# Output projection of a streaming-encoder block: additions moved between VectorE, ScalarE and GpSimd, two buffer pools merged, half of the weight sums traced later

## The chip, the cores and the metric

The kernel runs on one core of a Trainium2 chip. Its time is device microseconds of one execution. TensorE (PE) does the matrix products, VectorE (DVE), ScalarE (ACT) and GpSimd (POOL) the elementwise work, and SyncE (SP) issues nearly all transfers. Each engine works through its own list of instructions in the order in which the compiler has put them, and an instruction that waits holds everything behind it on the same engine.

## The reference, cut to what matters

One layer (depth 1) on a sequence of 2048 tokens with 1024 channels, all in float32:

```
mod = silu(c) @ ada_w + ada_b;  shift, scale, gate = split(mod, 3)
h   = rms_norm(x, norm_pre_w) * (1 + scale) + shift
z   = h @ w_in                                  # 1024 -> 6144 columns
pool_out = multiscale_pool(u) * silu(g_pool)    # 1024 channels
hgrn_out = rms_norm(hgrn2(q, f, i)) * silu(g_h) # 1024 channels, 8 heads
y   = concat(pool_out, hgrn_out) @ w_out        # 2048 -> 1024
out = x + gate * rms_norm(y, norm_post_w)
```

The change concerns the last two lines: the product with w_out, its two halves of the sum over the 2048 channels, the norm of y, and the addition of x.

## The kernel before, in words

Every large product is done in float32 quality from two rounded parts of each operand (`hi` and `lo`, made by `part`, L127: a ScalarE copy that rounds, then a VectorE subtraction), three matmuls for each product of parts. On top of that each block of two by two is computed with seven products instead of eight. `quad` (L356) does one such block: seven calls of `product` (L349), each 12 matmuls of 128 by 128 by 512, into three PSUM banks X, Z and Y, and seven additions that combine the banks into four results. The first copy of X goes to `c21` (L361). The first use of bank Z is copied by ScalarE into `c22` and `c21` is added by GpSimd (L368, L369). The others are VectorE additions of a bank to a tile (L372, L377, L380, L383). X itself is returned and left to the caller. The three banks (tag `ps_mm`) are shared by successive quads, so the next quad's first product waits until X has been read.

The kernel has these stages. A first part prepares the inputs. Then 48 steps, 24 for each half of the sequence, compute the columns of w_in head by head (`fq_step`, `hv_step`) and pool group by pool group (`pool_step`), with the attention units in between, and store the result in a scratch tensor `mix`. At last comes the output projection (from L844): 16 quads, eight with the pool half of the channels (`g` = 0, the first pass), whose results go to a scratch tensor `ypart`, and eight with the other half (`g` = 1, the second pass). A quad makes 256 rows of y, two tiles of 128 rows.

For each quad `mix_granule` (L743) loads 256 rows of `mix` into the one buffer `mraw` and makes seven operands (`m`, tag `w`, six buffers) with GpSimd sums (L758 to L766) and `part`. It is traced one quad ahead. The seven matching operands of w_out are made once for each pass by `load_out` (L718): 14 loads into `oraw` (tag `st`, two buffers), some from w_out itself, some from the scratch tensors `wos[0]` and `wos[1]`, and 28 pairs of a ScalarE and a VectorE instruction.

The sums of w_out that stand in `wos[g]` are made by `out_sums` (L702) in eight calls for each pass. One call loads two blocks of w_out into the tile `x` (tag `x1`, one buffer in all), scales them on ScalarE (L710), makes four GpSimd sums (L712 to L715) and stores the result (L716). The same single buffer `x1` serves `second_sums` in the first half, the gate's row in `gate_row` (L465), and at last the tile `gnb` that holds that row on all partitions (L844, L845). In the second half of the steps all 16 calls are traced, one with each `fq` and each `hv` step (L834), first the eight of pass 0, then `gate_row` (after head 3), then the eight of pass 1.

In the second pass each quad loads two tiles `yp` from `ypart` (L856) and adds them: VectorE adds X and its part (L867), GpSimd the other three quarters (L872; VectorE in the last quad). ScalarE sums the squares of a row tile (L877), GpSimd makes the reciprocal root (L111, L112), VectorE multiplies by it and by the gate's row (L881) and adds x (L882), and SP stores the result (L886). The tiles `yp` and `xf` (the x to be added) share three buffers (tag `px`).

The order of the instructions on each engine is not written by hand: a planner takes the traced program, gives earlier lines the higher priority, and puts on each engine, in a simulated timeline, the first instruction in priority that it thinks ready. An instruction traced late runs early if what it needs is free. The places marked `high_priority` are put ahead. Transfers are in the same way put in one order on SP.

Of the kernel before, what the change touches and what calls it, by code (L numbers as in the profile page):

```python
# [11 lines left out]
F32 = mybir.dt.float32  # L12
# [4 lines left out]
ALU = mybir.AluOpType  # L17
# [3 lines left out]
P = 128  # L21
D = 1024
# [5 lines left out]
BLK = 512  # L28
# [16 lines left out]
def build(nc, tc, a):  # L45
# [4 lines left out]
    out = a["out"][0]  # L50

    with tc.tile_pool(name="dram", bufs=1, space=DRAM) as dram, \
# [8 lines left out]
        gnrow = dram.tile([1, D], F32, name="gnrow")  # L61
# [72 lines left out]
        wsp = wsp_cm.__enter__()  # L134
# [13 lines left out]
        for m in (2, 4, 8, 16):  # L148
            n = 64 // m
# [14 lines left out]
        S = {}  # L164
# [190 lines left out]

        def quad(W, c12, c21, c22, begin=None):  # L356

            X, Z, Y = bank("mm"), bank("mm"), bank("mm")
# [8 lines left out]
            with tc.high_priority():  # L367
                nc.scalar.copy(c22, Z)  # L368
                nc.gpsimd.tensor_tensor(c22, c22, c21, ALU.add)  # L369
            product(Y, W[2], S["S2"], True)  # L370
# [347 lines left out]
        def load_out(g):  # L718

            r = {}  # L720
            for name, t in (("A11", None), ("S1", 0), ("S2", 3), ("A12", None), ("S3", 1), ("S4", None), ("A22", 2)):
                r[name] = []
                for j in range(2):
                    raw = fin[0].tile([P, 2, BLK], F32, name="oraw", tag="st", bufs=2)
                    hi, lo = s_tile("hi"), s_tile("lo")
# [85 lines left out]
        for i, step in enumerate(steps):  # L811
# [20 lines left out]
            if half == 0 and what == "pool" and n in (2, 4):  # L832
                second_sums(HEADS - 4 + n // 2 + 1)
            if half == 1 and what != "pool":  # L834
                out_sums(n // 4, n % 4, int(what == "hv"))
            if half == 1 and what == "hv" and n == 3:
# [6 lines left out]

        gn = wsp.tile([P, D], F32, name="gnb", tag="x1", bufs=1)  # L844
        nc.sync.dma_start(gn, gnrow[0].partition_broadcast(P))  # L845
        todo = [(g, p_) for g in range(2) for p_ in range(T // P // 2)]
        M = nxt
        for i, (g, p_) in enumerate(todo):
            if p_ == 0:
                S.update(O if g == 0 else load_out(1))  # L850
            nxt = mix_granule(*todo[i + 1]) if i + 1 < len(todo) else None
            y = [fin[0].tile([P, D], F32, name="y", tag="y", bufs=4) for _ in range(2)]
            if g:
                parts = [fin[0].tile([P, D], F32, name="yp", tag="px", bufs=3) for _ in range(2)]
                for t in range(2):
                    nc.sync.dma_start(parts[t], ypart[2 * p_ + t])  # L856
            X = quad(M, y[0][:, BLK:], y[1][:, 0:BLK], y[1][:, BLK:])
            M = nxt
            if g == 0:
                with tc.high_priority():  # L860
                    nc.scalar.copy(y[0][:, 0:BLK], X)
                for t in range(2):
                    nc.sync.dma_start(ypart[2 * p_ + t], y[t])
                continue
            final = i == len(todo) - 1
            with tc.high_priority():
                nc.vector.tensor_tensor(y[0][:, 0:BLK], X, parts[0][:, 0:BLK], ALU.add)  # L867
            for t in range(2):
                ts = slice((2 * p_ + t) * P, (2 * p_ + t + 1) * P)
                for n in ((1,), (1, 0))[t]:  # L870
                    ns = slice(n * BLK, (n + 1) * BLK)
                    (nc.vector if final else nc.gpsimd).tensor_tensor(y[t][:, ns], y[t][:, ns], parts[t][:, ns], ALU.add)  # L872
                xt = fin[0].tile([P, D], F32, name="xf", tag="px", bufs=3)
                nc.sync.dma_start(xt, x[ts])
# [4 lines left out]
                for n in range(2):  # L879
                    ns = slice(n * BLK, (n + 1) * BLK)  # L880
                    nc.vector.scalar_tensor_tensor(y[t][:, ns], y[t][:, ns], ss, gn[:, ns], ALU.mult, ALU.mult)  # L881
                    nc.vector.tensor_tensor(y[t][:, ns], y[t][:, ns], xt[:, ns], ALU.add)  # L882
                    if final:
                        nc.sync.dma_start(out[ts, ns], y[t][:, ns])
# [20 lines left out]
```

## Time and profile before

| what | value |
|---|---|
| median of 3 runs | 1822.91 us (1819.11 to 1823.12) |
| profiled execution, its own time | 1825.83 us |
| its span, first to last instruction | 1824.2 us |
| PE busy | 1650.4 us, 90% |
| DVE busy | 1118.2 us, 61% |
| POOL busy | 714.9 us, 39% |
| ACT busy | 645.0 us, 35% |
| mean granted TensorE clock | 0.951 |

Shares are of the span. "Idle before" an instruction is time in which its engine did nothing, and the name behind it is what ended the wait. The granted clock is a share of TensorE's full clock of 2.4 GHz: it takes two levels, full and half, and a mean between them over a stretch says how much of the stretch was at half. L numbers are lines of the kernel before.

### The profile page before, as it was taken

How to read it: one execution, taken by the hardware profiler on the slowest of the kernel's cores; microseconds unless marked ns; L12 is line 12 of the kernel's file. 1: busy time of each engine (PE TensorE's matmuls, PEld its weight loads, DVE VectorE, ACT ScalarE, POOL GpSimd, SP SyncE). 2: the span in 40 equal slices, each digit the busy share in tenths (PEclk: the TensorE clock that was granted, in tenths of full speed). 3: DMA queues.
4: the chain of work that ended last, by engine and by line, in shares of the span. 5: the costliest groups of instructions: out<-in, count | busy, mean ns of one | idle time of the engine just before them, and what ended most of it. 6: DMA issues, size and time to landing. Idle time of an engine off the chain costs nothing. (4 is left out here: it accounts for less than half of the span.)

```text
span 1824.2 us, 31561 instructions
## 1 busy us (share of the span) xinstructions
PE 1650.4 (90%) x12249; PEld 1302.8 (71%) x12249; DVE 1118.2 (61%) x1754; ACT 645.0 (35%) x1417; POOL 714.9 (39%) x924
## 2 busy tenths in 40 slices
PE   7779898999999699889998999989999899988896
PEld 6557676777777477677776877768787668866675
DVE  5496576676676466865545434445544874567776
ACT  4654243434443334443122222322122342343232
POOL 1374354547364627532212213432121233325563
PEclk8789999999999799999999999989999999999898
DMA  9636564667565647797532546554554563263454
GB/s 340 224 128 215 173 220 171 217 213 238 170 213 193 185 164 249 248 329 259 199 128 95 183 156 202 187 195 160 178 174 145 166 221 127 105 219 126 171 187 174
DMA packets 221475, 348.66 MB, mean 191 GB/s; under 512 B 45009, under 2 KB 152590, under 8 KB 221326
## 3 DMA queue, kind: packets, MB, share of 16 engines
q1 hardware_dynamic: 221240, 346.62, 56.5%
q8 instruction: 97, 1.59, 0.4%
q14 instruction: 52, 0.43, 0.1%
q10 hardware_dynamic: 86, 0.03, 0.0%
HBM read 203.99 MB, written 142.61 MB: 190 GB/s over the span
## 5 line engine op out<-in xcount | busy, mean ns | idle before, releaser
L353 PE MATMUL ps_mm<-hi,w 128*128 128x512 f32 x2304 | 786.6, 410 | 41.2 <-ACT ue L368 6.0
L353 PEld LDWEIGHTS ps_mm<-hi,w 128*128 128x128 f32 x2304 | 444.6, 194 | 149.1 <-ACT ue L368 7.1
L353 PE MATMUL ps_mm<-lo,w 128*128 128x512 f32 x1152 | 465.9, 405 | 12.3 <-DVE lo L130 9.1
L353 PE MATMUL ps_mm<-hi,m 128*128 128x512 f32 x896 | 292.8, 405 | 32.5 <-ACT m L129 9.4
L353 PEld LDWEIGHTS ps_mm<-lo,w 128*128 128x128 f32 x1152 | 224.4, 195 | 59.2 <-DVE lo L130 11.9
L353 PEld LDWEIGHTS ps_mm<-hi,m 128*128 128x128 f32 x896 | 174.5, 195 | 80.1 <-ACT m L129 11.9
L130 DVE TENSOR_TENSOR w<-wraw,w 128x512 fp32r<-128x512 f32 x168 | 141.8, 851 | 102.7 <-ACT w L129 94.6
L603 DVE TENSOR_TENSOR qk<-qk,tcn 128x512 f32<-128x512 f32 x192 | 148.7, 774 | 60.6 <-PE ps_lv L632 40.8
L353 PE MATMUL ps_mm<-lo,m 128*128 128x512 f32 x448 | 179.8, 402 | 2.4 <-DVE lo L736 1.8
L129 ACT CAST w<-wraw 128x512 fp32r<-128x512 f32 x168 | 101.9, 620 | 214.2 <-DMA wraw<-w_in 70.3
L353 PE MATMUL ps_mm<-hi,wpair 128*128 128x512 f32 x384 | 132.3, 406 | 5.1 <-DVE sg L501 4.7
L353 PEld LDWEIGHTS ps_mm<-lo,m 128*128 128x128 f32 x448 | 87.9, 196 | 21.9 <-DVE lo L736 3.0
L111 POOL TENSOR_SCALAR ss<-ss 128x4 f32<-128x4 f32 (+2 forms) x60 | 22.5, 375 | 187.1 <-ACT og L685 114.6
L611 PEld LDWEIGHTS ps_lv<-qk 128*32 128x32 f32 x4096 | 49.4, 113 | 55.2 <-issue 39.9
L353 PEld LDWEIGHTS ps_mm<-hi,wpair 128*128 128x128 f32 x384 | 72.9, 191 | 21.0 <-DVE sg L501 4.8
L611 PE MATMUL ps_lv<-qk 128*32 128x16 f32 x4096 | 63.7, 186 | 17.9 <-DVE qk L603 17.2
L130 DVE TENSOR_TENSOR m<-mraw,m 128x512 fp32r<-128x512 f32 x64 | 60.9, 963 | 30.8 <-ACT m L129 30.8
L324 POOL TENSOR_TENSOR wraw<-wraw 128x512 f32<-128x512 f32 x24 | 32.4, 1352 | 113.8 <-DMA wraw<-w_in 46.3
L353 PE MATMUL ps_mm<-lo,wpair 128*128 128x512 f32 x192 | 76.3, 397 | 0.0
L591 DVE COPY_PREDICATED diag<-mask,ps_lv 128x64 f32<-128x64 uint8 x128 | 30.8, 241 | 67.0 <-PE ps_lv L611 66.1
L554 POOL TENSOR_TENSOR tcn<-tcn 128x128 f32<-128x128 f32 (+4 forms) x160 | 65.7, 410 | 9.2
L554 POOL TENSOR_TENSOR tcn<-f 128x256 f32<-128x256 f32 x32 | 23.3, 727 | 114.0 <-ACT f L544 57.8
(279 smaller groups left out, 2640.8 us busy)
## 6 DMA issues: line engine op xcount, KB each, us to landing
wsd<-w SPq DMA_DIRECT2D x168, 512.0 KB
w<-wsd SPq DMA_DIRECT2D x120, 512.0 KB
wpair<-wsd SPq DMA_DIRECT2D x24, 1024.0 KB
wraw<-w_in SPq DMA_DIRECT2D x40, 512.0 KB
mraw<-mix SPq DMA_DIRECT2D x32, 512.0 KB
ada<-ada_w SPq DMA_DIRECT2D x16, 512.0 KB
mix<-g SPq DMA_DIRECT2D x32, 256.0 KB
mix<-sg SPq DMA_DIRECT2D x32, 256.0 KB
```

The costliest lines, as they stand in the source:

```text
L111: nc.gpsimd.tensor_scalar(ss, ss, inv, EPS, ALU.mult, ALU.add)
L129: nc.scalar.copy(hi, raw)
L130: nc.vector.tensor_tensor(lo, raw, hi.bitcast(F32), ALU.subtract)
L324: nc.gpsimd.tensor_tensor(B11, B12, B11, ALU.subtract)
L353: nc.tensor.matmul(ps, w[:, a_, k], s[k][b_], start=start and k == a_ == b_ == 0, stop=k == KH - 1 and a_ == 1, skip_group_check=not start)
L554: nc.gpsimd.tensor_tensor(dst, sv[:, :, 0], sv[:, :, 1], ALU.mult)
L591: nc.vector.copy_predicated(dst, mk, view(data, 0, [(16, NC_), (m, n), (1, m)]))
L603: nc.vector.tensor_tensor(dst, dst, t_, ALU.mult)
L611: nc.tensor.matmul(ps[q * 32:(q + 1) * 32, c * 16:(c + 1) * 16], K[:, t:t + 32], view(Q, t + m, [(2 * m, 16 // m), (1, m)]), start=True, s ...
```

## The change

- `quad` gets a flag `out`. With it, bank Z's first sum is one VectorE addition from the bank; without it, ScalarE copy and GpSimd addition as before. Only the 16 quads of the output projection set it.
- In both passes X is now copied to y by ScalarE. In the second pass the part of `ypart` for that quarter is added later, with the others, and all four quarter additions are on VectorE. The order of quarters is 0, 1 for the first row tile and 1, 0 for the second.
- The addition of x is on GpSimd, and on VectorE in the last quad only.
- `oraw` (two buffers) and `px` (three) become one tag with five buffers of the same size.
- `out_sums`: the second half's `hv` steps trace the eight calls of pass 0 (four before `gate_row`, four after it). The eight calls of pass 1 are traced in the quads of the first pass. `gnb` is taken at the start of the second pass.

```diff
-        def quad(W, c12, c21, c22, begin=None):
+        def quad(W, c12, c21, c22, begin=None, out=False):
...
-                nc.scalar.copy(c22, Z)
-                nc.gpsimd.tensor_tensor(c22, c22, c21, ALU.add)
+                if out:
+                    nc.vector.tensor_tensor(c22, Z, c21, ALU.add)
+                else:
+                    nc.scalar.copy(c22, Z)
+                    nc.gpsimd.tensor_tensor(c22, c22, c21, ALU.add)
...
-                    raw = fin[0].tile([P, 2, BLK], F32, name="oraw", tag="st", bufs=2)
+                    raw = fin[0].tile([P, 2, BLK], F32, name="oraw", tag="px", bufs=5)
...
-            if half == 1 and what != "pool":
-                out_sums(n // 4, n % 4, int(what == "hv"))
+            if half == 1 and what == "hv":
+                out_sums(0, n % 4, n // 4)
...
-        gn = wsp.tile([P, D], F32, name="gnb", tag="x1", bufs=1)
-        nc.sync.dma_start(gn, gnrow[0].partition_broadcast(P))
...
-                S.update(O if g == 0 else load_out(1))
+                S.update(load_out(1) if g else O)
+            if g and p_ == 0:
+                gn = wsp.tile([P, D], F32, name="gnb", tag="x1", bufs=1)
+                nc.sync.dma_start(gn, gnrow[0].partition_broadcast(P))
...
-                parts = [fin[0].tile([P, D], F32, name="yp", tag="px", bufs=3) for _ in range(2)]
+                parts = [fin[0].tile([P, D], F32, name="yp", tag="px", bufs=5) for _ in range(2)]
...
-            X = quad(M, y[0][:, BLK:], y[1][:, 0:BLK], y[1][:, BLK:])
+            X = quad(M, y[0][:, BLK:], y[1][:, 0:BLK], y[1][:, BLK:], out=True)
             M = nxt
+            with tc.high_priority():
+                nc.scalar.copy(y[0][:, 0:BLK], X)
             if g == 0:
-                with tc.high_priority():
-                    nc.scalar.copy(y[0][:, 0:BLK], X)
+                out_sums(1, p_ % 4, p_ // 4)
...
-            with tc.high_priority():
-                nc.vector.tensor_tensor(y[0][:, 0:BLK], X, parts[0][:, 0:BLK], ALU.add)
...
-                for n in ((1,), (1, 0))[t]:
+                for n in (t, 1 - t):
                     ns = slice(n * BLK, (n + 1) * BLK)
-                    (nc.vector if final else nc.gpsimd).tensor_tensor(y[t][:, ns], y[t][:, ns], parts[t][:, ns], ALU.add)
-                xt = fin[0].tile([P, D], F32, name="xf", tag="px", bufs=3)
+                    nc.vector.tensor_tensor(y[t][:, ns], y[t][:, ns], parts[t][:, ns], ALU.add)
+                xt = fin[0].tile([P, D], F32, name="xf", tag="px", bufs=5)
...
-                    nc.vector.tensor_tensor(y[t][:, ns], y[t][:, ns], xt[:, ns], ALU.add)
+                    (nc.vector if final else nc.gpsimd).tensor_tensor(y[t][:, ns], y[t][:, ns], xt[:, ns], ALU.add)
```

## Rows read from the trace of the kernel before

**Rows 1.** Stretches: us, busy us of PE PEld DVE ACT POOL, PEclk, DMA share, GB/s.
```profile
760.00:831.00 71.00, 63.92 (x300) 52.04 (x301) 48.60 (x76) 35.31 (x75) 25.32 (x34) 0.95 0.90 320
...
1110.00:1220.00 110.00, 95.73 (x864) 73.47 (x863) 51.63 (x96) 31.92 (x80) 48.32 (x62) 0.91 0.60 198
1220.00:1400.00 180.00, 179.82 (x1515) 143.87 (x1514) 85.85 (x159) 40.95 (x104) 35.97 (x57) 1.00 0.51 171
...
1457.00:1501.00 44.00, 38.59 (x148) 28.69 (x147) 33.56 (x46) 20.48 (x36) 13.41 (x10) 0.92 0.66 216
1501.00:1596.00 95.00, 95.00 (x421) 78.69 (x420) 47.92 (x58) 31.07 (x56) 33.82 (x26) 1.00 0.33 122
1596.00:1645.00 49.00, 40.94 (x170) 32.19 (x169) 34.73 (x47) 22.90 (x41) 12.78 (x10) 0.97 0.61 204
1645.00:1815.00 170.00, 147.77 (x588) 116.15 (x587) 126.14 (x148) 50.90 (x91) 93.38 (x83) 0.93 0.49 170
```

**Rows 2.** Waits from 1110 to 1220 us: who for whom, us, times, longest.
```profile
ACT x L710 <- DMA x<-w_out: 59.8, 8, 13.3
...
PE ps_mm L353 <- DVE sg L501: 4.7, 1, 4.7
```

**Rows 3.** ScalarE in order of time, 1114 to 1136 us: start, us, instruction, [idle before].
```profile
1131.89 1.36 ACT L710 ACTIVATE x<-x,vec 128x512 f32<-128x512 f32 x2 [13.32 <-DMA x<-w_out]
...
1133.85 0.57 ACT L368 COPY ue<-ps_mm 128x512 f32<-128x512 f32 x1
```

**Rows 4.** All of L710: duration least/median/most in ns, first and last start.
```profile
L710 ACT ACTIVATE x<-x,vec x32: 704/722/751, 698.1 to 1209.9; 128x512 f32<-128x512 f32 x32
```

**Rows 5.** SyncE's transfers in order of issue, 1186 to 1222 us.
```profile
1215.74 0.37 SPq L716 DMA_DIRECT2D wos<-x  x1
...
1219.58 0.33 SPq L845 DMA_DIRECT2D gnb<-gnrow  x1
```

**Rows 6.** Waits of TensorE from 1608 us to the end.
```profile
PE ps_mm L353 <- ACT m L129: 9.4, 6, 2.8
PE ps_mm L353 <- DVE y L372: 9.0, 4, 4.3
PE ps_mm L353 <- DVE y L867: 8.7, 2, 6.3
```

**Rows 7.** Groups of instructions from 1350 us: busy us, mean ns | idle before, releasers.
```profile
L881 DVE SCALAR_TENSOR_TENSOR y<-y,ss,gnb 128x512 f32<-128x512 f32 x32 | 38.6, 1240 | 5.2 <-POOL ss L112 5.2
L872 POOL TENSOR_TENSOR y<-y,yp 128x512 f32<-128x512 f32 x21 | 32.3, 1540 | 32.6 <-DVE y L383 25.1 <-DVE y L380 6.2 <-DVE y L377 1.1
...
L882 DVE TENSOR_TENSOR y<-y,xf 128x512 f32<-128x512 f32 x32 | 25.4, 816 | 0.3 <-DMA xf<-x 0.3
...
L369 POOL TENSOR_TENSOR y<-y 128x512 f32<-128x512 f32 x16 | 22.6, 1410 | 48.2 <-ACT y L368 48.2
...
L867 DVE TENSOR_TENSOR y<-ps_mm,yp 128x512 f32<-128x512 f32 x8 | 5.5, 686 | 16.1 <-PE ps_mm L353 8.1 <-DMA yp<-ypart 4.8 <-issue 3.3
...
L861 ACT COPY y<-ps_mm 128x512 f32<-128x512 f32 x8 | 4.7, 582 | 1.6 <-PE ps_mm L353 1.6
```

**Rows 8.** VectorE in order of time, 1685 to 1699 us.
```profile
1690.42 1.48 DVE L130 TENSOR_TENSOR m<-S,m 128x512 fp32r<-128x512 f32 x1 [3.22 <-ACT m L129]
1691.83 0.68 DVE L867 TENSOR_TENSOR y<-ps_mm,yp 128x512 f32<-128x512 f32 x1
```

**Rows 9.** VectorE in order of time, 1772 to 1778 us.
```profile
1772.84 2.44 DVE L881 SCALAR_TENSOR_TENSOR y<-y,ss,gnb 128x512 f32<-128x512 f32 x2 [0.44 <-POOL ss L112]
1775.19 1.28 DVE L882 TENSOR_TENSOR y<-y,xf 128x512 f32<-128x512 f32 x2
1776.40 0.68 DVE L130 TENSOR_TENSOR m<-mraw,m 128x512 fp32r<-128x512 f32 x1
```

**Rows 10.** SyncE's transfers in order of issue, 1775 to 1780 us.
```profile
1776.51 0.34 SPq L886 DMA_DIRECT2D out_dram<-y  x1
...
1777.42 1.24 SPq L747 DMA_DIRECT2D mraw<-mix  x2
```

## The prediction

> **What bounds the kernel now.** I read the stretches first. Between 1501 and 1596 us, in the first pass, TensorE is busy for 95.00 of 95.00 us at full clock: 421 matmuls, five quads, so 19.0 us a quad and 2.7 us a product [rows 1]. That is the floor, and the change touches none of these matmuls, so only what TensorE loses elsewhere can be won. I count a loss as idle time plus half of the time at half clock, which the mean clock of a stretch gives (0.91 means 18% of the stretch at half, so 9% lost). By that the first pass's start (1457 to 1501) loses 5.4 + 3.5 = 8.9 us, the change of passes (1596 to 1645) 8.1 + 1.5 = 9.6, the second pass (1645 to 1815) 22.2 + 11.9 = 34.1, and, in the second half's steps, 1110 to 1220 loses 14.3 + 9.9 = 24.2, while 1220 to 1400 loses 0.2 [rows 1]. In the second pass an idle microsecond is thus followed by another 0.54 at half clock (11.9 / 22.2).
>
> Then I asked who ended the waits. In the second pass there are three: ScalarE's rounding of a `mix` operand (9.4 us), VectorE's L372 (9.0) and L867 (8.7) [rows 6]. Between 1110 and 1220 it is the sums of w_out: ScalarE stood eight times, 59.8 us in all, before L710 until the block had landed [rows 2]. How that reaches TensorE is seen in order of time: 13.32 us of idle, the two L710, and only then the copy of a bank at 1133.85 that the next product waits for [rows 3]. VectorE's L501, which costs TensorE 4.7 us there, waits for ScalarE in the same way [rows 2].
>
> **The change, part by part.** The sum is made against the profiled execution, 1825.8 us with 1824.2 of span.
>
> *Sums of w_out in the steps.* The trace order is moved, but not the chain: one buffer `x1`, always passed to the next user in trace order. The planner runs such work as soon as the buffer is free. `gnb`, traced after all steps, was issued at 1219.58, right behind the last sum's store at 1215.74 [rows 5], and the first sum, traced in the second half, ran at 698 [rows 4]. There are 32 L710, two a call; eight calls lie in 1110 to 1220 [rows 2], hence eight before 831. What stands between is `gate_row`, which holds `x1` until its matmuls are placed with head 3. After the change four calls precede it, and twelve follow: the other four of pass 0 and, by the same pull, the eight of pass 1, although they are traced in the first pass. So I expect twelve where there were eight, from 1110 to some 1270 us (an estimate, 110 / 8 = 13.8 us a call), into a stretch that now loses nothing. Price: 24.2 / 8 = 3.0 us a call, four more calls, **+12 us**. Ends: 0 if they fall beside nothing urgent, as 1220 to 1400 shows without them; +28 if each costs 7, twice and more the mean, as when a wait of 13 us is hit; -12 if the new order is as much kinder to the four pass 0 calls that remain.
>
> *The four calls that leave 760 to 831.* That stretch loses 7.1 + 3.6 = 10.6 us [rows 1]. Besides the sums it holds the loading of the second half's operands, and into it now come the 16 VectorE instructions of `gate_row` with their 16 loads. **-3 us**; ends -10.6 and +5, half of the same loss again.
>
> *Five shared buffers.* `oraw` can be loaded five deep instead of two, with nothing else in these buffers in the first pass. SP then stands less often before an `oraw` load, behind which the load of `mraw` waits. But the 28 roundings for each pass need operand buffers that come free only product by product, so most of the work stays where it is. First pass's start: **-3** of 8.9; change of passes: **-4** of 9.6. Ends: everything (-8.9 and -9.6), or +2 each where five loads at once slow the one of `mraw`.
>
> *Bank Z's first sum on VectorE.* 16 additions with a bank as one input, 0.69 us each by L867's form [rows 7], for 16 POOL additions of 1.41 us (and as many ScalarE copies). In the first pass VectorE is busy 47.9 of 95 us [rows 1], so it hides: 0. Z takes further products only later, so nothing waits for the older pair either.
>
> *X by ScalarE, partials on VectorE, residual on POOL.* For each quad of the second pass VectorE loses L867 (0.69) and four L882 (0.82 each) and gains Z's sum (0.69) and four partials of the same shape as L882; POOL loses L369 (1.41) and three L872 (1.54) and gains four residuals that I price like L872: 6.0 against 6.2. ScalarE exchanges a copy for one of 0.58 [rows 7]. The load of each engine stays; only the order can pay. Three effects:
> X no longer waits for VectorE. At 1691.83 L867 ran at once when VectorE reached it, behind a rounding that had itself waited 3.22 us [rows 8]; TensorE's longest wait, 6.3 us, ended there, and 2.4 us more on L867 elsewhere [rows 6]. ScalarE copies X in its place at 0.58. Late next is that rounding: it ends at 1691.9, and the second product needs it, which in the old order came 2.7 us after 1692.65. So 3.5 of the 6.3 are won, and the 2.4 whole: 5.9, with the clock behind them 9.1. ScalarE also stands behind late `mix` tiles, so I take -8.
> L372 waits among VectorE's own additions; partials come there as residuals go. -1, ends 0 and -7 (4.7 of its 9.0 lie in the second pass proper, times 1.54).
> The load of `mraw` waits for the last rounding of the granule ahead, which on VectorE stood behind two L881 and two L882: 2.44 and 1.2 us until 1776.40 [rows 9]. Without the residuals it comes 1.2 us sooner. But on SP the load stood behind the store of the finished rows (1776.51, then 1777.42) [rows 10], and that now waits for POOL. I give half of it: -3.
> Together **-12 us**; ends -34 (all of the loss) and +16 (below).
>
> The two row sets that a rule bears on: VectorE's additions with one input in a bank took 0.69, those with both in SBUF 0.82 and 1.24 on average [rows 7]. The Trainium skill says why, on the page SBUF — State Buffer, section Who interferes with whom: a VectorE instruction with two SBUF inputs and a GpSimd one that reads SBUF shut each other out for a whole instruction, one with at most one SBUF input doesn't. By the rule the partials move onto VectorE as additions that a residual on POOL can hold up, which speaks against this part, while Z's sum can't be held up and takes eight POOL additions of 1.41 out of the second pass. By the row alone the exchange is zero; by the rule VectorE could be up to 8 x 1.41 = 11 us shorter there, off the path for the most part, so that the sum would be lower by 1 or 2.
>
> *The tail.* The last quad's residual stays on VectorE, so the chain behind the last product is the old one: 0.
>
> Sum: 12 - 3 - 3 - 4 - 8 - 1 - 3 = -10, so 1815.8 us for a profiled execution. The median of the three runs lies 2.9 us under the profiled one, so I say **1813 us**.
>
> **The rivals.**
> *The sums stay in the first pass.* If the planner does not pull the eight calls of pass 1 forward, the second half keeps four calls instead of eight: -12 where I put +12, so 1789. For it: the first pass has idle ScalarE and POOL [rows 1]. The last call then belongs to the last quad, and its 13.8 us can hold up the operand S1 of pass 1 by up to those: 1789 to 1803, say 1796. Against it: `gnb` [rows 5].
> *Nothing that can be measured.* The engines' loads are equal, and if TensorE's waits only change their names, the second pass keeps its 34 us: 12 - 3 - 7 = +2, so 1825.
> *Slower: the residual on POOL holds up SP.* The store of a row tile is issued when the addition of x is done. On POOL that addition takes some 1.5 us and can stand behind one of the next granule's sums, of the same length. Where SP has the store ahead of the load of `mraw`, as at 1776.51 [rows 10], each such quad gets its operands 1.5 us later, and with the clock TensorE loses 2.3. In seven quads that is +16, in half of them +8 in place of -12: 12 - 10 + 8 = +10, 1833. It decides from two quads on, if nothing else in the second pass is won. For it: the order store, then `mraw` is in the trace. Against it: POOL is also rid of the partials, which waited for TensorE's last bank for 25.1 us [rows 7].
>
> **How the numbers follow.** About 0.3%, 5.5 us, is what a measurement of this kernel can tell from no change. My forecast gets 0.42, its own range 1805 to 1822, of which 0.32 is faster than 1817.4. The sums in the first pass get 0.13, all faster. No change gets 0.20: 0.02 faster, 0.14 the same, 0.04 slower. The POOL rival gets 0.25: 0.02 the same, 0.23 slower. Faster 0.32 + 0.13 + 0.02 = 0.47, the same 0.10 + 0.14 + 0.02 = 0.26, slower 0.27. The range 1796 to 1834 leaves out half of the first rival and a part of the third, some 0.15.
>
> **What would show it.** In the changed profile: twelve calls of `out_sums` after `gate_row`, the last before 1300 us, and TensorE's losses from 1110 to 1280 near 36 us; no wait on L867's successor above 3 us; ScalarE's waits for `oraw` shorter; VectorE's and POOL's busy time in the second pass within 5% of the old. The forecast is wrong if sums run beside the first pass's quads, if the store of rows holds SP longer than VectorE's did, or if the losses after 1596 us stay near 44.

## The result and the profile after

The changed kernel takes 1804.64 us (median of four runs, 1800.54 to 1806.18) against 1823.01 us: ratio 0.9891, 95% interval 0.9855 to 0.9926, a gain of 1.1%, with 0.4 to either side. The profiled execution took 1806.18 us with a span of 1804.2, where the one of before took 1825.8 with 1824.2. The forecast of 1813 was too careful by 8 us. The range of 1796 to 1834 holds the time; the narrower 1805 to 1822 that I gave to the forecast's own path misses it by 0.4 us.

To say where the 20 us between the two profiles went I cut each trace by quads: every quad is 84 matmuls of L353 (seven products of 12), 48 quads belong to the steps and 16 to the output projection (48 to 55 the first pass, 56 to 63 the second), and the table gives the time from the start of one quad's first matmul to that of another's (in the last column, to the start of the last matmul). The bottom two lines are means over kernels that share one order of instructions in these columns: the kernels with the old places of the sums (before, e2 to e5, e9, e10) and those with the new (after, e1, e6, e7).

```
quads           0-22   22-26  26-35  35-42  42-46  46-50  50-54  54-56   56-64  span
                                                   first  first  change  second
                                                   start  pass           pass
before          670.5  116.9  245.3  201.9  95.3   112.3  76.2   46.2    190.6  1824.2
after           668.9  114.9  240.2  203.3  95.3   112.3  77.3   41.8    182.0  1804.2
old sums, mean         117.3  244.8  200.0  95.3
new sums, mean         113.4  241.8  204.2  95.3
```

The gain lies in the second pass (-8.6), at the change of passes (-4.4) and in two stretches of the steps (22-26, from which four calls of `out_sums` went, and 26-35, where the chain of loads of `gate_row` no longer runs); 35-42, which took in four more calls, lost a little. The columns to 22 are the same work in the same order in all fourteen kernels, and yet took 663.9 to 674.2 us from profile to profile. A single profile thus says nothing of a few microseconds of the whole; a stretch is read by the mean of several kernels, and the whole by ratios. The last two columns spread less where kernels have the same order of instructions there: 182.0 to 183.0 us in the second pass (after, e4, e11, e12) and 41.6 to 41.8 at the change (after, e4, e6), though 39.2 and 41.4 in e11 and e12.

The stretches after, counterpart of [rows 1], with the same columns (the first four: the old place of the four calls; the twelve calls' first eight; their last four; what follows them; the last three: the start of the first pass, the first pass, the change of passes):

```profile
757.00:824.00 67.00, 62.49 (x299) 50.44 (x299) 53.05 (x86) 29.34 (x59) 14.65 (x15) 0.94 0.87 305
1101.00:1210.00 109.00, 94.69 (x865) 72.48 (x864) 52.11 (x97) 31.75 (x80) 48.15 (x62) 0.94 0.61 200
1210.00:1262.00 52.00, 49.66 (x407) 39.70 (x407) 23.83 (x43) 14.98 (x34) 21.75 (x31) 1.00 0.73 237
1262.00:1391.00 129.00, 128.82 (x1101) 102.71 (x1100) 61.51 (x114) 30.63 (x78) 26.70 (x42) 1.00 0.52 172
1450.00:1493.00 43.00, 36.63 (x150) 29.45 (x149) 31.53 (x46) 12.61 (x23) 11.27 (x8) 0.92 0.53 171
1493.00:1590.00 97.00, 95.76 (x422) 78.65 (x421) 46.76 (x62) 28.46 (x49) 27.59 (x21) 1.00 0.28 104
1590.00:1637.00 47.00, 40.96 (x174) 31.99 (x173) 37.23 (x53) 24.72 (x44) 12.86 (x8) 1.00 0.79 255
```

Between 1101 and 1210 TensorE loses 14.3 us to idleness, as it did with eight calls before [rows 1]; the four calls more (1210 to 1262) cost 2.3 us at full clock. The first pass's start is as before: 6.4 idle at a clock of 0.92, where it was 5.4 at 0.92 [rows 1].

The second pass, quads 56 to 64 of either kernel, first before, then after, same columns:

```profile
1623.00:1814.00 191.00, 167.48 (x674) 131.91 (x672) 141.05 (x168) 61.24 (x109) 99.25 (x87) 0.94 0.51 176
```

```profile
1612.00:1794.00 182.00, 160.98 (x672) 126.69 (x672) 140.68 (x166) 59.05 (x106) 102.23 (x88) 0.98 0.54 181
```

Of the 9.0 us that these two differ by, 2.5 are idleness of TensorE (23.5 to 21.0) and 6.5 are busy time of the same matmuls: the granted clock went from 0.94 to 0.98, so the part of the pass at 1.2 GHz fell from 12% to 4%. VectorE, ScalarE and POOL are as busy as they were. What changed is how the idle time is cut up. The waits of TensorE from the same point on as [rows 6], after:

```profile
PE ps_mm L353 <- DVE y L380: 9.2, 6, 1.9
PE ps_mm L353 <- DVE y L375: 5.6, 3, 2.7
PE ps_mm L353 <- ACT m L129: 4.0, 3, 1.5
PE ps_mm L353 <- DVE m L130: 4.0, 4, 1.6
PE ps_mm L353 <- DVE y L369: 0.4, 1, 0.4
```

(L375 is the old L372, L380 the old L377, L369 bank Z's sum.) In the second pass five waits of before were over 2 us, up to 6.3; after, one is, of 2.7. The sums of w_out, and `gnb`, in SyncE's order of issue [rows 4, 5]:

```profile
L713 ACT ACTIVATE x<-x,vec x32: 704/722/746, 696.5 to 1253.4; 128x512 f32<-128x512 f32 x32
```

```profile
1258.12 0.37 SPq L719 DMA_DIRECT2D wos<-x  x1
...
1261.34 0.32 SPq L854 DMA_DIRECT2D gnb<-gnrow  x1
```

The last sum starts at 1253 us, although the eight calls of pass 1 are written in the first pass of the projection, which begins at 1381.

### The profile page after: what moved, and what is told of

Read it like the earlier page. It is cut to its first block, busy times and chain, and to the rows that moved or that the text cites. A ratio compares the mean times of both kernels' runs of the same rounds, so it can differ in the third digit from the quotient of the medians.

```text
span 1804.2 us, 31567 instructions
## 1 busy us (share of the span) xinstructions
PE 1637.2 (91%) x12249; PEld 1294.7 (72%) x12249; DVE 1116.9 (62%) x1763; ACT 640.4 (35%) x1409; POOL 713.4 (40%) x915
## 4 chain that ended last, share of the span: by engine, by line
PE 41%; DMA 16%; DVE 15%; POOL 12%; issue 9%; ACT 6%; SPq 1%; POOLq 0%; DVEq 0%; ACTq 0%
PE ps_mm L353 33%; DMA wraw<-w_in 3%; DMA x<-w_out 3%; DVE m L130 2%; DVE w L130 2%; DMA wos<-x 2%; PE ps_lv L614 1%; DVE lo L130 1%; DVE qk L606 1%; ACT w L129 1%; POOL wraw L324 1%; PE ps_o L681 1%; DVE y L884 1%; POOL wraw L327 1%; DMA wraw<-wup 1%
## 5 line engine op out<-in xcount | busy, mean ns | idle before, releaser
L353 PE MATMUL ps_mm<-hi,w 128*128 128x512 f32 x2304 | 786.0, 410 | 39.0 <-ACT ue L371 5.4
L353 PEld LDWEIGHTS ps_mm<-hi,w 128*128 128x128 f32 x2304 | 444.0, 194 | 146.3 <-ACT ue L371 6.5
L353 PE MATMUL ps_mm<-lo,w 128*128 128x512 f32 x1152 | 466.2, 405 | 12.5 <-DVE lo L130 9.4
L353 PE MATMUL ps_mm<-hi,m 128*128 128x512 f32 x896 | 286.2, 398 | 32.4 <-DVE y L380 9.2
L353 PEld LDWEIGHTS ps_mm<-lo,w 128*128 128x128 f32 x1152 | 223.3, 194 | 59.6 <-DVE lo L130 12.4
L353 PEld LDWEIGHTS ps_mm<-hi,m 128*128 128x128 f32 x896 | 170.2, 191 | 79.6 <-ACT m L129 10.6
L130 DVE TENSOR_TENSOR w<-wraw,w 128x512 fp32r<-128x512 f32 x168 | 140.5, 844 | 107.2 <-ACT w L129 91.5
L606 DVE TENSOR_TENSOR qk<-qk,tcn 128x512 f32<-128x512 f32 x192 | 153.0, 797 | 61.2 <-PE ps_lv L635 39.8
L353 PE MATMUL ps_mm<-lo,m 128*128 128x512 f32 x448 | 177.0, 395 | 0.0
L353 PE MATMUL ps_mm<-hi,wpair 128*128 128x512 f32 x384 | 132.0, 404 | 4.0 <-DVE sg L504 3.6
L353 PEld LDWEIGHTS ps_mm<-lo,m 128*128 128x128 f32 x448 | 85.5, 191 | 17.4
L353 PEld LDWEIGHTS ps_mm<-hi,wpair 128*128 128x128 f32 x384 | 73.0, 191 | 19.9 <-DVE sg L504 3.7
L614 PE MATMUL ps_lv<-qk 128*32 128x16 f32 x4096 | 64.2, 186 | 17.6 <-DVE qk L606 17.5
L353 PE MATMUL ps_mm<-lo,wpair 128*128 128x512 f32 x192 | 76.1, 397 | 0.0
L130 DVE TENSOR_TENSOR m<-mraw,m 128x512 fp32r<-128x512 f32 x64 | 62.0, 976 | 19.9 <-ACT m L129 19.9
L130 DVE TENSOR_TENSOR m<-S,m 128x512 fp32r<-128x512 f32 x48 | 44.1, 918 | 42.8 <-ACT m L129 41.9
```

The costliest lines, as they stand in the source:

```text
L130: nc.vector.tensor_tensor(lo, raw, hi.bitcast(F32), ALU.subtract)
L353: nc.tensor.matmul(ps, w[:, a_, k], s[k][b_], start=start and k == a_ == b_ == 0, stop=k == KH - 1 and a_ == 1, skip_group_check=not start)
L606: nc.vector.tensor_tensor(dst, dst, t_, ALU.mult)
L614: nc.tensor.matmul(ps[q * 32:(q + 1) * 32, c * 16:(c + 1) * 16], K[:, t:t + 32], view(Q, t + m, [(2 * m, 16 // m), (1, m)]), start=True, s ...
```

## The experiments

Each ratio is to runs of the kernel before on the same chip (medians 1821.4 to 1823.2 us), with its 95% interval. The stages are in the units of the table above, the last three columns of which I give as start, change and second pass.

### The places of the sums

**e1.** Before, with the new places of the sums and of `gnb` alone:

```
-            if half == 1 and what != "pool":
-                out_sums(n // 4, n % 4, int(what == "hv"))
+            if half == 1 and what == "hv":
+                out_sums(0, n % 4, n // 4)
...
+                out_sums(1, p_ % 4, p_ // 4)      # first pass
```

> The kernel before with the new places of out_sums and gnb alone. By the prediction's price (+12 for four more calls after gate_row, -3 before it) it is 9 us slower than before. By my reading of the changed kernel's trace the extra calls cost far less than 3 us each: 0 to -3 us against before. The rival (the sums' new places carry the gain, since the changed profile reaches the output projection 6 us earlier) says -6 or more.

Measured: 1817.82 us, 0.9973 (0.9956 to 0.999): a gain of 3.6 us by the medians where my sum for this part was +9. The sums are pulled forward as in the changed kernel, and 22-26 and 26-35 become shorter by as much as 35-42 becomes longer, or more.

**e4.** After, with the old places of the sums (the reverse of e1):

> The changed kernel with out_sums and gnb in their places of before. Theory: -13 to -16 us, nearly all of the 18 that were measured for the whole change. If the sums' new places carry the gain: -9 or less. If buffers and additions need each other, this is more than the two runs with one part alone add up to.

Measured: 1807.82 us, 0.9907 (0.988 to 0.9935). The intervals of this and of the changed kernel overlap almost whole; its change of passes (41.7) and second pass (182.0) are those of the changed kernel. So what is gained there is none of the sums' doing.

**e8.** After, with the eight calls of pass 1 kept in the first pass, each behind the load of a `mix` granule, one a quad:

```
         mixed = []
         def mix_granule(g, p_):
-                nc.sync.dma_start(raw[:, i], mix...)
+                mixed.append(nc.sync.dma_start(raw[:, i], mix...).ins)
...
-                out_sums(1, p_ % 4, p_ // 4)
+                with tc.issue_after(mixed[-1]):
+                    out_sums(1, p_ % 4, p_ // 4)
```

> The changed kernel with the eight calls of pass 1 really in the first pass: SP may issue their transfers only behind the load of mraw of their own quad. Theory (a call costs TensorE time in the steps, by the changed trace 17.6 us for eight calls and 2.3 for the last four): 6 to 12 us faster than the changed kernel, -25 to -31 against before, minus up to 5 at the change of passes, where the last call's result is needed. Rival (the losses from 1101 to 1210 belong to the steps there and not to the calls): 0 to -3 against the changed kernel.

Measured: 1793.41 us, 0.9835 (0.981 to 0.986), the fastest kernel of all; its six runs (1782.59 to 1799.28) all lie under the four of the changed one, and the two intervals only just meet. Its stretches 35-42, 50-54 and the second pass, columns as in [rows 1]:

```profile
1086.00:1273.00 187.00, 181.19 (x1589) 143.89 (x1589) 95.62 (x177) 48.82 (x124) 54.73 (x80) 0.99 0.53 176
1482.00:1558.00 76.00, 76.00 (x337) 62.93 (x336) 36.85 (x50) 26.22 (x46) 41.82 (x36) 1.00 0.46 162
1599.00:1787.00 188.00, 164.31 (x671) 127.56 (x670) 151.65 (x178) 67.08 (x119) 104.12 (x89) 0.96 0.59 207
```

35-42 falls from 204.2 (mean with twelve calls) to 186.6, 17.6 us for eight calls. The first pass takes one call a quad for nothing: TensorE is busy 76.00 of 76.00 us. The second pass gives 6.5 back (188.5 for 182.0). The last call's store is issued at 1600.4 us, when the second pass has begun, and a part of w_out is late behind it, as TensorE, then ScalarE in order of time show:

```profile
1608.50 0.80 PE L353 MATMUL ps_mm<-hi,m 128*128 128x512 f32 x1 [3.94 <-ACT hi L129]
```

```profile
1607.83 1.14 ACT L129 CAST hi<-oraw 128x512 fp32r<-128x512 f32 x2 [5.16 <-DMA oraw<-wos]
```

**e11.** e8 with two calls in each of the first four quads, so that the last ends early:

```
-                    out_sums(1, p_ % 4, p_ // 4)
+                    for q in (2 * p_, 2 * p_ + 1) if p_ < 4 else ():
+                        out_sums(1, q % 4, q // 4)
```

> The changed kernel with the eight calls of pass 1 held in the first pass, two in each of its first four quads, so that the last result is there three quads before it is needed. With one a quad TensorE waited 3.9 us for an operand of pass 1 and the second pass took 188.5 us. Theory: that wait and the half clock behind it go, second pass 182 us, 4 to 6 us faster than with one a quad, -33 to -36 against before. Rival (two calls a quad delay the granules of the first pass, or the second pass's order is just another): no gain, -25 to -30.

Measured: 1805.22 us, 0.9911 (0.9884 to 0.9938). The change of passes (39.2) and the second pass (182.2) are mended, but 50-54 takes 95.3 us instead of 76.2. That stretch, and ScalarE's waits in it:

```profile
1479.00:1574.00 95.00, 83.86 (x336) 66.59 (x335) 36.59 (x49) 28.04 (x48) 43.47 (x41) 0.93 0.51 173
```

```profile
ACT m L129 <- DMA mraw<-mix: 22.6, 4, 8.2
ACT x L713 <- DMA x<-w_out: 19.5, 7, 5.3
```

So there is room for one call a quad, not for two: ScalarE then stands in front of L713 and waits longer for `mraw` (in e8 the two waits are 2.5 and 11.2 us in its stretch). The rival of the expectation, that two calls a quad delay the granules, is the one that came.

**e12.** e11 with all eight calls of pass 0 ahead of `gate_row`:

```
-            if half == 1 and what == "hv":
-                out_sums(0, n % 4, n // 4)
+            if half == 1 and what != "pool" and n < 4:
+                out_sums(0, n, int(what == "hv"))
```

> The same with all eight calls of pass 0 ahead of gate_row, as before the change. The stretch where four calls followed gate_row gets 3 to 8 us shorter, the one before it 4 us longer (117.0 against 113.3 in the runs so far): 0 to -4 us against two a quad. Rival (four calls behind gate_row cost nothing): 4 us slower than that.

Measured: 1810.07 us, 0.9938 (0.9917 to 0.9959). Without any call 35-42 is 183.8 us long, 3.9 less than with the four of e11, but 22-26 and 26-35 are 3.8 longer together (6.9 by the means of the table). From the first pass on both kernels have the same order of instructions, so the 2.2 and 0.8 us by which the change of passes and the second pass are longer are spread. The gain of 0 to 4 us that I expected didn't come; the median is 4.9 above that of e11, near the 4 of the rival, and the intervals overlap. These four calls are no cheaper ahead of `gate_row`.

### The buffers

**e2.** Before, with the five shared buffers alone:

```
-  raw = fin[0].tile(..., name="oraw", tag="st", bufs=2)
+  raw = fin[0].tile(..., name="oraw", tag="px", bufs=5)
-  ... name="yp", tag="px", bufs=3        ... name="xf", tag="px", bufs=3
+  ... name="yp", tag="px", bufs=5        ... name="xf", tag="px", bufs=5
```

> The kernel before with oraw, yp and xf in five shared buffers and nothing else. Theory (each part pays by itself): the start of the first pass and the change of passes get 5 us shorter, the second pass 0 to 3: -5 to -8 us in all. Rival (the buffers pay only with the additions moved, since partials on POOL release them late): 0 to -2.

Measured: 1812.43 us, 0.9954 (0.9935 to 0.9974). First start 112.5, change of passes 45.9, second pass 186.3: nothing where I had put the gain, and 4.3 us where I had put 0 to 3. The whole, 8.4 us by the ratio, is near what I expected, and 4 us more than these stages show; where the rest lies isn't shown. TensorE's waits for VectorE from 1595 us on:

```profile
PE ps_mm L353 <- DVE y L372: 19.9, 8, 5.3
...
PE ps_mm L353 <- DVE y L867: 1.2, 2, 0.7
```

With more buffers for `yp` and `xf` the wait for X's sum goes from 8.7 [rows 6] to 1.2 us by itself, and L372 takes its place.

### The additions

**e3.** Before, with the additions of the change, three and two buffers, and the old sums:

```
+                if out:
+                    nc.vector.tensor_tensor(c22, Z, c21, ALU.add)
...
+            with tc.high_priority():
+                nc.scalar.copy(y[0][:, 0:BLK], X)
...
-                    (nc.vector if final else nc.gpsimd)...  # partials
+                    nc.vector...
-                    nc.vector...                            # residual
+                    (nc.vector if final else nc.gpsimd)...
```

> The kernel before with Z's first sum, the copy of X, the partials and the residual on their new engines, the buffers and the sums as before. Theory: the second pass (from the first product of its second quad to the last) gets 8 us shorter, change of passes 0 to -2: -8 to -10 us. Rival: with three buffers the partials on VectorE wait for yp and stand before its bank sums, so that nothing is won: 0 or slower.

Measured: 1810.08 us, 0.994 (0.9918 to 0.9962); second pass 182.9, change of passes 45.7. The additions alone bring 7.7 of the 8.6 us of the second pass and next to nothing at the change. The change falls only where buffers and additions meet (e4: 41.7; e2 45.9, e3 45.7); which addition that is, e7 below tells.

**e5.** Before, with X copied by ScalarE in both passes and its partial added on POOL like the other three:

```
+            with tc.high_priority():
+                nc.scalar.copy(y[0][:, 0:BLK], X)
-            with tc.high_priority():
-                nc.vector.tensor_tensor(y[0][:, 0:BLK], X, parts[0][:, 0:BLK], ALU.add)
-                for n in ((1,), (1, 0))[t]:
+                for n in (t, 1 - t):
```

> The kernel before with one edit: in the second pass X is copied by ScalarE and its part of ypart is added by GpSimd like the other three. Theory (L867 on VectorE held bank X): TensorE no longer waits 8.7 us there, the second pass gets 5 to 8 us shorter, -4 to -7 us against before. Rival (the wait goes over to what is late next, L372 and the mix operands; and GpSimd gets 8 more additions of 1.5 us): 0 to -2 us, with the waits on L372 grown by what went.

Measured: 1831.01 us, 1.0045 (1.0027 to 1.0063), slower; second pass 198.7 us. The step to which I gave most costs 8 us by itself. TensorE's waits from 1604 us on:

```profile
PE ps_mm L353 <- DVE y L372: 24.9, 8, 5.5
PE ps_mm L353 <- ACT m L129: 8.7, 4, 3.3
```

L867 is gone, and L372, 9.0 us before [rows 6], holds 24.9.

**e9.** Before, with the three partials on VectorE and L867 kept:

```
-                    (nc.vector if final else nc.gpsimd).tensor_tensor(y[t][:, ns], y[t][:, ns], parts[t][:, ns], ALU.add)
+                    nc.vector.tensor_tensor(y[t][:, ns], y[t][:, ns], parts[t][:, ns], ALU.add)
```

> The kernel before with the three partials of each quad of the second pass on VectorE instead of GpSimd; X plus its part stays one VectorE addition from the bank. Theory (partials on GpSimd, which waits for TensorE's last bank with the next granule's sums queued behind them, make the second pass late): second pass 190.6 to 182 to 185 us, -6 to -9 in all. Rival (the gain needs X off VectorE): second pass 188 or more; VectorE, with 8 residuals, partials and L867, becomes the bound and it is slower.

Measured: 1820.73 us, 0.9996 (0.9979 to 1.0012); second pass 187.0 in the one profile, no difference in the whole. TensorE's waits from 1609 us on:

```profile
PE ps_mm L353 <- DVE y L867: 13.3, 5, 5.1
PE ps_mm L353 <- DVE y L372: 8.6, 3, 4.0
```

**e10.** e5 and e9 together, X by ScalarE and all four partials on VectorE:

> The kernel before with X copied by ScalarE and all four partials on VectorE (residual on VectorE, Z's sum, buffers and sums as before). With X by ScalarE alone the second pass took 198.7 us. If the partials' engine decides: 182 to 186 us. If the move of X is a loss by itself (8 us), it stays 5 us or more above the run with the partials alone.

Measured: 1820.89 us, 0.9997 (0.9981 to 1.0014); second pass 190.6, that of the kernel before to a tenth. TensorE's waits from 1604 us on:

```profile
PE ps_mm L353 <- DVE y L372: 22.4, 7, 6.5
PE ps_mm L353 <- ACT m L129: 4.1, 4, 1.7
```

From e10 to e3 (190.6 to 182.9) only the residual goes to POOL and Z's sum to VectorE. These two are taken back singly, in the changed kernel. No run has the residual on POOL with X and the partials in their old places, so whether it needs their move is open.

**e6.** After, with the residual on VectorE:

```
-                    (nc.vector if final else nc.gpsimd).tensor_tensor(y[t][:, ns], y[t][:, ns], xt[:, ns], ALU.add)
+                    nc.vector.tensor_tensor(y[t][:, ns], y[t][:, ns], xt[:, ns], ALU.add)
```

> The changed kernel with the addition of x back on VectorE in all quads. Theory (the gain in the second pass is from less work on VectorE between the last product and the release of mraw; moving four additions of 0.8 us per quad back takes VectorE from 124 to some 147 of 158 us): 5 to 10 us slower than the changed kernel, so -10 to -15 against before. The rival of the prediction (residuals on GpSimd hold up the stores on SP and behind them the load of mraw) says faster than the changed kernel: -20 or more against before.

Measured: 1808.3 us, 0.9918 (0.99 to 0.9936), which overlaps the changed kernel's interval; second pass 184.5 (182.0), change of passes 41.6. Of the 5 to 10 us that I expected 2.5 stand in the second pass; the whole can't tell it from none. The waits show what the residual moves. First ScalarE's and SyncE's for `mix`, after, from 1597 us on (SyncE's L889 is the store of the rows, L750 the load of `mraw`):

```profile
ACT m L129 <- DMA mraw<-mix: 13.7, 8, 5.1
```

```profile
SPq L889 <- POOL y L885: 97.8, 14, 9.3
SPq L750 <- DVE m L130: 12.1, 8, 2.1
```

Then the same waits, and TensorE's longest, in e6 from 1591 us on:

```profile
ACT m L129 <- DMA mraw<-mix: 36.6, 8, 6.8
```

```profile
SPq L889 <- DVE y L885: 86.4, 10, 12.1
SPq L750 <- DVE m L130: 34.9, 8, 6.9
```

```profile
PE ps_mm L353 <- DVE y L375: 19.1, 9, 3.2
```

The price that I had put on it, VectorE busier by 23 us, did not come. The second pass of e6, columns as in [rows 1], and all of its residuals (least, median, most in ns, first and last start):

```profile
1606.00:1791.00 185.00, 165.60 (x675) 131.25 (x673) 136.18 (x195) 59.49 (x106) 61.57 (x60) 0.94 0.53 178
```

```profile
L885 DVE TENSOR_TENSOR y<-y,xf x32: 676/680/686, 1635.9 to 1796.9; 128x512 f32<-128x512 f32 x32
```

VectorE runs 195 instructions instead of 166 and is busy for 136.2 us instead of 140.7, since its other additions become shorter: in the second pass the partials (L875) take 0.71 us on average, where they took 0.89 with the residual on POOL, and the subtractions of L130 from `mraw` 0.70, where they took 1.15.

**e7.** After, with Z's first sum copied by ScalarE and added on POOL:

```
-            X = quad(M, ..., out=True)
+            X = quad(M, ...)
```

> The changed kernel with bank Z's first sum as before (ScalarE copy, GpSimd addition). Theory by the row (nobody waits for that sum, its load is small): within 3 us of the changed kernel, -16 to -20 against before. Theory by the shared access to SBUF (a GpSimd addition holds up VectorE's additions with two SBUF inputs): 3 to 8 us slower than the changed kernel, with a longer mean of L130 and L884 in the second pass.

Measured: 1808.24 us, 0.9926 (0.9908 to 0.9943), again overlapping the changed kernel; second pass 181.3, change of passes 44.3 instead of 41.8. TensorE's waits from 1597 us on:

```profile
PE ps_mm L353 <- DVE y L375: 10.0, 5, 4.0
PE ps_mm L353 <- DVE y L380: 8.3, 5, 1.9
```

So Z's sum adds nothing in the second pass. At the change of passes it does. There e7 has the same order of instructions as e2, with the buffers and without Z's sum: 44.3 and 45.9 us. The three kernels with the buffers and Z's sum on VectorE that share one order there (after, e4, e6) take 41.6 to 41.8. TensorE's longest wait in that stretch is half as long. In order e2 (1564.3 to 1610.1 us), e7 (1568.3 to 1612.5) and after (1570.5 to 1612.3):

```profile
PE ps_mm L353 <- DVE y L372: 4.0, 1, 4.0
```

```profile
PE ps_mm L353 <- DVE y L375: 4.0, 1, 4.0
```

```profile
PE ps_mm L353 <- DVE y L375: 2.5, 2, 2.1
```

The granted clock in these three stretches was 0.93, 0.96 and 1.00.

## Why the prediction came out as it did

**The sums are pulled forward: right.** Twelve calls stand behind `gate_row`, eight of them traced a whole pass later, and the last starts at 1253 us; I had said before 1300.

**Four more calls, +12: the size was wrong.** Measured +4.2 (200.0 to 204.2). ScalarE's waits before the sums did grow with the calls, from 59.8 us [rows 2] to this, from 1101 to 1262 us:

```profile
ACT x L713 <- DMA x<-w_out: 89.1, 13, 13.8
```

But TensorE pays for such a wait when something that it needs is next behind it on ScalarE, as the copy in [rows 3]. Behind the last four calls that happened twice, and these two waits are all the 2.3 us of idleness from 1210 to 1262:

```profile
1243.08 0.50 PE L353 MATMUL ps_mm<-hi,w 128*128 128x512 f32 x1 [0.76 <-ACT f L361]
...
1254.42 0.49 PE L679 MATMUL ps_o<-v,attn 128*128 128x128 f32 x2 [1.58 <-ACT attn L636]
```

The clock did not fall there. By the prediction's own count the stretch of all twelve calls loses 14.3 + 6.5 + 2.3 = 23 us, where I had said near 36. A mean price per call, 3.0, was the wrong unit for calls added at the end. It was not far off for calls taken away: e8 got 2.2 for each of eight.

**Four calls out of 760 to 831, -3: right,** -3.9 in the means. A term was missing. With four calls ahead of it instead of eight, the chain of loads and additions of `gate_row` runs earlier, before and after:

```profile
L476 DVE SCALAR_TENSOR_TENSOR gn<-adag,sc,gn x14: 750/752/1025, 844.7 to 894.5; 128x512 f32<-128x512 f32 x14
```

```profile
L479 DVE SCALAR_TENSOR_TENSOR gn<-adag,sc,gn x14: 739/747/1250, 771.7 to 850.0; 128x512 f32<-128x512 f32 x14
```

So nearly all of it leaves 26-35 (846 to 1091 us before), and that stretch is 3.0 us shorter; that the one is the cause of the other is argued.

**The first pass's start, -3 by buffers: wrong,** 0.0 in the changed kernel and +0.2 in e2, although ScalarE's waits for `oraw` fell as I had said. From 1457 to 1645 us before, and then from 1450 to 1637 after, they are:

```profile
ACT hi L129 <- DMA oraw<-wos: 12.8, 8, 3.1
ACT hi L735 <- DMA oraw<-w_out: 8.9, 5, 2.6
```

```profile
ACT hi L129 <- DMA oraw<-wos: 2.8, 2, 2.3
```

ScalarE's waits for TensorE to free operand buffers grew instead, between the same times from 7.3 to 32.2 us for `m` and from nothing to 5.3 for `hi`. That fits the bound that I had named, that the roundings wait for such buffers anyway; no run tests it by itself.

**The change of passes, -4 by buffers: the size right (-4.4), the cause not.** Buffers alone gave -0.3, additions alone -0.5, both -4.5 (e2, e3, e4). The addition that counts is Z's sum, which I had priced at 0: buffers without it give 45.9 and 44.3 us (e2, e7), with it 41.6 to 41.8.

**The second pass, -12 in three steps: measured -8.6, and the step that carried it failed.** "X no longer waits for VectorE", -8: e5 shows +8.1 with the partials on POOL, e10 shows 0.0 with them on VectorE. I had looked at one instruction, L867, and priced the wait that ended in it. The products wait for whichever of VectorE's instructions frees the next bank, and VectorE's queue was no earlier for having one reader of a bank less: as L867's 8.7 us went, L372's grew from 9.0 to 22.4 and 24.9. Why e5 is even slower isn't settled; that four partials a quad on POOL hold up the rows is only argued.

"The load of `mraw` waits for the rounding behind the residuals", -3: here the residual was the right place, and its size depends on the buffers. ScalarE's wait for `mraw` in the second pass, and SyncE's for its buffer (L747, now L750), in us:

```
residual on VectorE   before 42.8 19.9   e1 41.9 21.2   e2 33.4 29.3   e5  34.0 30.0
                      e6     36.6 34.9   e9 23.4 26.0   e10 22.8 27.1
residual on POOL      after  13.7 12.1   e3  5.2 11.9   e4 12.0 11.9   e7  16.5 13.7
                      e8     10.3 18.0
```

By the first number twelve kernels fall into two groups with the engine of the residual alone. It is worth 7.7 us without the five buffers (e10 to e3, where Z's sum, which e7 finds at nothing in the second pass with the buffers, went along) and 2.5 with them (e6 to after): buffers (e2, -4.3) and residual do not add up. That TensorE gains by these waits is argued: e10 has 20.0 us less of ScalarE's than before, and the same second pass. I had taken the gain to be idleness removed, with 0.54 of clock behind each microsecond. The clock's part was larger. In the four kernels with the second pass of the changed one (after, e4, e11, e12) 2.5 to 4.1 us of idleness went against before, and 3.5 to 6.2 us of busy time.

**Engine loads the same, additions by their inputs.** VectorE's and POOL's busy time is within 4% of the old, as forecast. The rule on the page SBUF — State Buffer (Who interferes with whom) of the Trainium skill agrees with the rows after. All of Z's sum, with one input in a bank, then the partials with both in SBUF, then the residual on POOL (least, median, most in ns):

```profile
L369 DVE TENSOR_TENSOR y<-ps_mm,y x16: 676/679/692, 1455.4 to 1780.1; 128x512 f32<-128x512 f32 x16
```

```profile
L875 DVE TENSOR_TENSOR y<-y,yp x32: 678/693/1777, 1623.7 to 1795.4; 128x512 f32<-128x512 f32 x32
```

```profile
L885 POOL TENSOR_TENSOR y<-y,xf x28: 1286/1731/1754, 1639.2 to 1787.5; 128x512 f32<-128x512 f32 x28
```

The first kind hardly varies, the second goes up to 1.78 us. With the residual off POOL (e6) the same partials took at most 1.28, and VectorE was less busy with 28 additions more, so the residuals on POOL cost VectorE's other instructions more (some 23 us, an estimate from 140.7, 136.2 and 28 times 0.68) than they take on VectorE. By the rule the sum would have been lower by 1 or 2 through Z's sum; e7 shows none of it in the second pass, though VectorE was busy there for 144.7 us with Z's sum on POOL and 140.6 without.

**The rivals.** That the sums stay in the first pass did not happen, but e8 made it happen, and its 1793 is near the 1796 worked out for it. That nothing changes is refuted (0.9891, interval up to 0.9926). That the residual on POOL makes the kernel slower is refuted too, though not its first step. SyncE's wait before the store was 93.8 us, in the line of before, and 97.8 after; between kernels that differ by the residual it grew by 11.4 and 12.3 (e6 to after, 86.4 to 97.8; e10 to e3, with Z's sum, 85.0 to 97.3). But ScalarE's wait for `mraw` fell. A longer hold of SyncE, which I had named as a sign that the forecast is wrong, was a bad sign.

```profile
SPq L886 <- DVE y L882: 93.8, 13, 14.7
```

The stages as measured add up to 4.2 - 3.9 - 3.0 + 0 - 4.4 - 8.6 = -15.7, and the two medians differ by 18.4. My -10 came as near as it did because errors ran against each other: 8 too much for the sums, and 3 for their effect on `gate_row` not seen, against 3 at the first start that did not come and 3 too many in the second pass. That the time lies in the range is thus in part luck. **What stays open:** why the residual's engine changes TensorE's waits when VectorE is no less busy for it, and whether its gain needs X and the partials moved. A version with one call a quad, begun a quad or two earlier, might keep what e8 gains without its 6.5 us at the end; it was not tried.

## What to carry to other kernels

A wait that ends in one instruction is not priced by that instruction: where the engine's queue is late, taking the instruction off it hands the wait to the next one, so ask what would make the queue itself earlier (here the work ahead of the roundings, and buffers for what it reads). Work without a deadline that is written late may run early and be paid for there; tie it to something that happens late, one piece to each stretch with room, and look at what needs its last piece. Try parts of a change together as well as singly: of the buffers and the additions each gained alone in the second pass and the two did not add up there, while at the change of passes neither gained alone and both together did. And before work is moved off an engine, ask what it will cost that engine from where it goes: the residuals on POOL slowed VectorE's other additions.

## What the runs showed of the hardware

The same instructions in the same order took 663.9 to 674.2 us over the first 22 quads, in fourteen profiled executions.

Many short waits were cheaper than a few long ones of nearly the same sum. In the second pass 23.5 us of TensorE's idleness went with a mean granted clock of 0.94 before, with five waits over 2 us, and 23.7 us with 0.96 in e8, with one; e6 and e12 idle for 19.4 us each, with five such waits and 0.94, and with none and 0.96. Over all fourteen kernels the clock of the second pass was 0.93 to 0.95 with two waits over 2 us or more, e7 apart (two, of 2.1 and 2.4, and 0.97), and 0.96 to 0.98 with one or none.

In the changed kernel VectorE's 128x512 f32 additions with both inputs in SBUF (L875) took 0.68 to 1.78 us beside additions on POOL, those with one input in a PSUM bank (L369) 0.68 to 0.69. And 28 such additions that went over from POOL to VectorE (after to e6) left VectorE busy for 136.2 us of the second pass instead of 140.7.
